# Stick-breaking scores copied to SBUF by ACT, sums in place, and a unit's turned weights asked for one unit later with a third buffer

## Chip, cores and metric

One Trainium2 chip, one core. The metric is the device time of one execution in microseconds (us), the median of three runs. Lower is better.

## What is computed

One layer of a hybrid decoder on 512 tokens of width 2048, in float32. A combined projection of the normalised input gives two groups of 16 heads of 64: group A is sliding-window attention, group B is stick-breaking attention. Both outputs are normalised, go through one output projection and are added to the input; an MLP with a squared ReLU (2048 to 8192 to 2048) follows. The change touches group B, which is this for each head:

```
z        = q . k / sqrt(64)                       # 512 x 512, strictly causal
log_beta = log_sigmoid(z)
log_1m   = where(causal, log_sigmoid(-z), 0)
later    = cumsum(log_1m, reversed) - log_1m      # along the keys
w        = where(causal, exp(log_beta + later), 0)
out      = w @ v
```

## The kernel before

Every large product is made of three TensorE products of float32r parts (`mm3`, lines 123 to 125): each operand is split by ACT (the high part, line 91) and DVE (the low part, line 92). The time has four stages: group A's and B's projections and attention, the output projection (`out_group`, tiles `ps_o`), the up products (`ps_u`) and the down products (`ps_d`).

The attention has no stage of its own. It is spread between the products of the projections. A group of products (`group_T`, `v_group`, `out_group`) calls `pump()` after every 12 of them; a call is a tick here. On odd ticks `pump` begins a unit if one is due, on even ticks it ends an earlier one. A unit of group B (`sb_pair`) is one block of 128 queries of a pair of heads (s = 0 and 1), so that a pair has four units, i = 0 to 3, with w = 128, 256, 384 and 512 keys.

- `begin(i)`: six products give the scores `z` (line 558) of both heads, in two PSUM banks. ACT makes Abs, Exp and Ln (lines 571 to 573), DVE max(z, 0) + Ln (line 574, reading `z`), POOL masks the diagonal block (line 575), DVE scans from the end (line 578) and subtracts the sum from the scores (line 580, reading `z` once more), POOL masks again (line 581), and ACT takes Exp (line 583). The result is tile `b`.
- `end(i)`: TensorE turns the weights by transposes (`wtr`, line 592), DVE copies them to SBUF (`wt`, line 593). After i = 3 the weights meet the values (`bv`, line 609), and `finish_o` takes the squares and stores the output.

`pa` has four PSUM banks. The scores, the turned weights, `bv` and the small products of other helpers take them in turn, so a unit's scores take the two banks of the unit before, and the turned weights the two between. A bank is given out again when its last reader is done: for the scores that is line 580. A unit is ended on the tick after the next one has begun, which is three ticks after its own beginning. Within a group of 16 ticks eight units run, that is two pairs; the units of one pair of pairs begin 11 ticks after its q and k are projected. In the tick where a group of projections ends, its q and k are also evacuated by DVE (line 328), split by ACT (line 323) and POOL (line 324).

The order of instructions on each engine is fixed before the run by a planner. It starts from the order of the program but may put later instructions first where it reckons that an earlier one has to wait.

Of the kernel before, what the change touches and what calls it, by code (L numbers as in the profile page):

```python
# [12 lines left out]
F32 = mybir.dt.float32  # L13
F32R = mybir.dt.float32r
AF = mybir.ActivationFunctionType
ALU = mybir.AluOpType
# [4 lines left out]
P = 128  # L21
T = 512
# [36 lines left out]
def hymba_layer(ctx: ExitStack, tc: tile.TileContext, x, norm_attn_g, w_in, q_norm_g, k_norm_g,  # L59
                sinks, rel_bias, swa_out_g, sb_out_g, w_out, norm_mlp_g, w_up, w_down, sel, eye, out):  # L60
    nc = tc.nc
    x, out = x[0], out[0]
# [21 lines left out]
    wk = attn.enter_context(tc.tile_pool(name="wk", bufs=2, side="right"))  # L84
# [44 lines left out]
    nc.scalar.dma_start(out=ident, in_=eye)  # L129
    NG = 50  # L130
    gT = const.tile([P, NG], F32, name="gT")
    gin = wk.tile([16, P], F32, tag="wb", name="gin")
    nc.scalar.dma_start(out=gin, in_=norm_attn_g.rearrange("o (k p) -> (o k) p", p=P))


# [26 lines left out]

    def xsquares(n, xb):
        for t in range(NT):
            junk = wk.tile([P, 512], F32, tag="wd", name=f"jx{n}_{t}")
            nc.scalar.activation(out=junk, in_=xb[:, t], func=AF.Square, accum_out=ss1[:, t, n:n + 1])

    kv_parts = []
# [45 lines left out]
    nc.vector.memset(c15, 1.5)  # L214
    ones2 = const.tile([P, 2], F32, name="ones2")
    nc.vector.memset(ones2, 1.0)
    bo32 = wk.tile([P, P], F32, tag="wb", name="bo32")
    nc.vector.memset(bo32, 0.0)
    for s in range(2):
        nc.vector.memset(bo32[s * DH:(s + 1) * DH, s * DH:(s + 1) * DH], 1.0 / DH)  # L220
# [56 lines left out]
    chains, units, flight, clock = [], deque(), deque(), [0]  # L277
# [5 lines left out]
    def pump():  # L283
        clock[0] += 1
        chains[:] = [g for g in chains if next(g, None) is not None]
        if clock[0] % 2:
            begun = bool(units) and units[0][0] <= clock[0]
            if begun:
                begin, end = units.popleft()[1]
                begin()  # L290
                flight.append(end)
            flight.append(None) if not begun and flight else None
        elif len(flight) > 1:
            end = flight.popleft()
            if flight[0] is None:
                flight.clear()
            end()

    def drain():
        while units or flight:  # L300
# [30 lines left out]
    def normed(ps, gcol, name):  # L331


        qf = evacuated(ps, 1.0, name)
        o = qkp.tile([P, 2, T], F32R, tag="qk", name=f"hl_{name}")

        def chain():
            sq = wk.tile([P, T], F32, tag="wb", name=f"sq_{name}")
            nc.scalar.square(out=sq, in_=qf)
            sh = wk.tile([P, T], F32R, tag="wc", name=f"sh_{name}")  # L340
            nc.scalar.copy(out=sh, in_=sq)
            sl = wk.tile([P, T], F32R, tag="wd", name=f"sl_{name}")
            nc.vector.tensor_tensor(out=sl, in0=sq, in1=sh.bitcast(F32), op=ALU.subtract)
            for _ in range(CHAIN):
                yield True
            mp = bank(f"mp_{name}")
            nc.tensor.matmul(mp, bo, sh, start=True, stop=False)
            nc.tensor.matmul(mp, bo, sl, start=False, stop=True)
            y = wk.tile([P, T], F32, tag="wc", name=f"y_{name}")
            t1 = wk.tile([P, T], F32, tag="wd", name=f"qt_{name}")  # L350
            nc.scalar.activation(out=y, in_=mp, func=AF.Ln, scale=LN_SCALE, bias=epsb)
            nc.scalar.activation(out=y, in_=y, func=AF.Exp, scale=-0.5, bias=lnb)
            nc.scalar.square(out=t1, in_=y)
            nc.vector.scalar_tensor_tensor(out=t1, in0=mp, scalar=EPS, in1=t1, op0=ALU.add, op1=ALU.mult)
            nc.scalar.activation(out=t1, in_=t1, func=AF.Identity, scale=-0.5, bias=c15)
            nc.vector.scalar_tensor_tensor(out=qf, in0=qf, scalar=gT[:, gcol:gcol + 1], in1=y,
                                           op0=ALU.mult, op1=ALU.mult)
            nc.vector.tensor_tensor(out=qf, in0=qf, in1=t1, op=ALU.mult)
            hilo(qf, o)

        g = chain()
        next(g)
        chains.append(g)
        return o
# [60 lines left out]
    def swa_pair(g, m, q, turned):  # L425
        c = 4 * g + m
# [26 lines left out]
        def softmax(hf, sc):  # L453
            prs = []
            bt = bias[0]
            for s in range(2):
                h = heads[s]
                pr = wk.tile([P, 2, 256], F32, tag=("wa", "wb")[s], name=f"pr{c}_{hf}{s}")
                scv = sc[s].rearrange("p (n k) -> p n k", n=2)
                if hf == 0:  # L460
                    nc.gpsimd.memset(pr[:, 0, 0:P], NEG)
                    nc.vector.tensor_tensor(out=pr[:, 0, P:], in0=scv[:, 0, P:], in1=bt[:, s, P:], op=ALU.add)
                    nc.vector.tensor_tensor(out=pr[:, 1], in0=scv[:, 1], in1=bt[:, s], op=ALU.add)
                else:
                    nc.vector.tensor_tensor(out=pr, in0=scv,
                                            in1=bt[:, s:s + 1].broadcast_to([P, 2, 256]), op=ALU.add)
                mx = sm.tile([P, 2], F32, tag="mx", name=f"mx{c}_{hf}{s}")
                nc.vector.tensor_reduce(out=mx, in_=pr, axis=AX.X, op=ALU.max)
                nm = sm.tile([P, 2], F32, tag="nm", name=f"nm{c}_{hf}{s}")
                nc.vector.tensor_scalar(out=nm, in0=mx, scalar1=sink[:, h:h + 1], scalar2=-1.0,  # L470
                                        op0=ALU.max, op1=ALU.mult)
                den = sm.tile([P, 2], F32, tag="den", name=f"den{c}_{hf}{s}")
                es = sm.tile([P, 2], F32, tag="es", name=f"es{c}_{hf}{s}")
                for nn in range(2):
                    nc.scalar.activation(out=pr[:, nn], in_=pr[:, nn], func=AF.Exp, bias=nm[:, nn:nn + 1],
                                         accum_out=den[:, nn:nn + 1])
                nc.scalar.activation(out=es, in_=nm, func=AF.Exp, bias=sink[:, h:h + 1])
                nc.vector.tensor_tensor(out=den, in0=den, in1=es, op=ALU.add)
                nc.vector.reciprocal(out=den, in_=den)
                for nn in range(2):  # L480
                    nc.gpsimd.tensor_scalar(out=pr[:, nn], in0=pr[:, nn], scalar1=den[:, nn:nn + 1],
                                            scalar2=1.0, op0=ALU.mult, op1=ALU.mult)
                prs.append(pr)
            return prs
# [31 lines left out]
                                         start=(j == 0), stop=(j == 3))  # L516
                finish_o(av, 0, 4 * g + 2 * s + m // 2)

        return [(partial(begin, hf), partial(end, hf)) for hf in range(2)]

    qperm = (lambda st: st.rearrange("p (s m d) -> p m s d", s=2, m=4, d=DH),
             lambda st: st.rearrange("p (m s d) -> p m s d", s=2, m=4, d=DH))
# [26 lines left out]
    def sb_pair(c, q, k, vs, keep):  # L549
# [12 lines left out]
        def weights(i, sc):  # L562
            w = (i + 1) * P
            dg = slice(i * P, (i + 1) * P)
            ws = []
            for s in range(2):
                z = sc[s][:, 0:w]
                a = wk.tile([P, 512], F32, tag=("wa", "wc")[s], name=f"a{c}_{i}{s}")[:, 0:w]
                b = wk.tile([P, 512], F32, tag=("wb", "wd")[s], name=f"b{c}_{i}{s}")[:, 0:w]

                nc.scalar.activation(out=a, in_=z, func=AF.Abs)
                nc.scalar.activation(out=a, in_=a, func=AF.Exp, scale=-1.0)
                nc.scalar.activation(out=a, in_=a, func=AF.Ln, bias=1.0)
                nc.vector.scalar_tensor_tensor(out=b, in0=z, scalar=0.0, in1=a, op0=ALU.max, op1=ALU.add)
                nc.gpsimd.affine_select(out=b[:, dg], in_=b[:, dg], pattern=[[-1, P]], compare_op=ALU.is_gt,
                                        fill=0.0, base=0, channel_multiplier=1)

                nc.vector.tensor_tensor_scan(out=a[:, ::-1], data0=ones2[:, 0:1].broadcast_to([P, w]),
                                             data1=b[:, ::-1], initial=0.0, op0=ALU.mult, op1=ALU.add)
                nc.vector.tensor_tensor(out=b, in0=z, in1=a, op=ALU.subtract)  # L580
                nc.gpsimd.affine_select(out=b[:, dg], in_=b[:, dg], pattern=[[-1, P]], compare_op=ALU.is_gt,
                                        fill=NEG, base=0, channel_multiplier=1)
                nc.scalar.activation(out=b, in_=b, func=AF.Exp)
                ws.append(b)
            return ws
# [27 lines left out]
            if o is not None:  # L613
                ohl[1, c] = o

        return [(partial(begin, i), partial(end, i)) for i in range(4)]

    ohl = {}

# [5 lines left out]
    for o in range(2):  # L625
        vs = v_group(o)
        for hq in range(2):
# [12 lines left out]
            for pr, (q, k) in enumerate(((q0, k0), (q1, k1))):  # L640
                c = 2 * qd + pr
# [284 lines left out]
    wd = w_down.rearrange("(g r p) n -> r p g n", r=2, p=P)  # L926
# [135 lines left out]
    for cj in range(2 * NC):  # L1062
        c, j = divmod(cj, 2)
# [7 lines left out]
        for s, (name, ai, _, b, more) in enumerate(d_products(cj)):  # L1071
# [33 lines left out]
            if not more:  # L1105
                pool, tag = ((pa, "pa"), (pp, "pp"))[b // 2]
                banks[b] = [pool.tile([P, 512], F32, tag=tag, name=f"ps_d{q}{tt}") for tt in range(2)]
            a = act[c, ai]

            at_end = q == 14 * NC - 1  # L1110
            for h, tt in sorted(((h, tt) for h in range(2) for tt in range(2)), key=lambda x: x[::-1] if at_end else x):
# [3 lines left out]
                for kk in range(2):  # L1115
                    al, ar = a[:, 0, 2 * h + kk, ts], a[:, 1, 2 * h + kk, ts]
                    first, end = h == 0 and kk == 0 and not more, h == 1 and kk == 1
# [36 lines left out]
```

## Time and profile before

| | |
|---|---|
| median of 3 runs | 1998.48 us (1997.99 to 2000.78) |
| the profiled execution's own time | 1998.97 us |
| its span, first to last instruction | 1997.2 us |
| TensorE busy | 1976.4 us, 99% |
| DVE, ACT, POOL busy | 1649.4, 1037.5, 1011.3 us |
| group B's units, first scores to last `bv` | about 320 to 629 us of the span |

A span is time on the core; the run's own time is 1.8 us longer. Products overlap each other by a part of their duration, so that two products of 0.39 us follow each other every 0.23 us. A gap is therefore best read from start to start.

### The profile page before, as it was taken

The page shows a single profiled execution, that of the slowest core. Times are in us where ns is not written, and L with a number is a line of the kernel's source. Part 1 is how long each engine was busy: PE and PEld are TensorE (multiplying, and loading weights), DVE is VectorE, ACT ScalarE, POOL GpSimd, SP SyncE. Part 2 cuts the span into 40 slices and gives each one's busy share as a digit, 9 for nine tenths or more (in the row PEclk, how much of TensorE's full clock was granted, in tenths as well). Part 3 has the DMA queues.
Part 4 walks back from the last instruction along what each step waited for, and adds up shares of the span by engine and source line. Part 5 has one row for each costly group of instructions (what it writes and reads, how often), then busy time and mean ns, then how long its engine had stood idle before and what let it go on. Part 6 is the DMA issues. An engine that isn't in the chain of part 4 may idle for free.

```text
span 1997.2 us, 31358 instructions
## 1 busy us (share of the span) xinstructions
PE 1976.4 (99%) x11652; PEld 1717.5 (86%) x11652; DVE 1649.4 (83%) x2142; ACT 1037.5 (52%) x1900; POOL 1011.3 (51%) x898
## 2 busy tenths in 40 slices
PE   8999999999999999999999999999999999999999
PEld 7887787778777889999999999998888888888887
DVE  4469654664776479999999999999999999999997
ACT  6357544453554575656565656565443333333444
POOL 0013431221321038777777777776866656656653
PEclk9999999999999999999999999999999999999999
DMA  6732332224245555665656565656766457456451
GB/s 224 146 119 80 100 98 83 75 69 137 93 140 172 192 169 180 217 201 189 208 181 215 180 216 181 212 176 245 290 250 250 158 221 291 161 221 261 143 204 67
DMA packets 213916, 350.31 MB, mean 175 GB/s; under 512 B 9779, under 2 KB 154372, under 8 KB 206596
## 3 DMA queue, kind: packets, MB, share of 16 engines
q1 hardware_dynamic: 211216, 345.02, 51.0%
q10 hardware_dynamic: 2548, 3.30, 1.3%
q8 instruction: 91, 1.49, 0.3%
q14 instruction: 61, 0.50, 0.1%
HBM read 270.16 MB, written 78.12 MB: 174 GB/s over the span
## 4 chain that ended last, share of the span: by engine, by line
PE 89%; DVE 5%; ACT 3%; POOL 1%; issue 1%; DMA 1%; POOLq 0%; SPq 0%; DVEq 0%; ACTq 0%
PE ps_u L831 11%; PE ps_u L830 11%; PE ps_u L832 11%; PE ps_d L1119 9%; PE ps_d L1120 9%; PE ps_d L1118 9%; PE ps_qk L123 3%; PE ps_qk L125 3%; PE ps_qk L124 3%; PE ps_o L125 2%; PE ps_o L123 2%; PE ps_o L124 2%; PE ps_qa L123 1%; PE ps_qa L124 1%; PE ps_qa L125 1%; DVE lo_d L92 1%
## 5 line engine op out<-in xcount | busy, mean ns | idle before, releaser
L832 PE MATMUL ps_u<-h2h,lo_u 128*128 128x256 f32 x1792 | 507.5, 283 | 0.1
L830 PE MATMUL ps_u<-h2h,hi_u 128*128 128x256 f32 x1792 | 507.6, 283 | 0.0
L831 PE MATMUL ps_u<-h2l,hi_u 128*128 128x256 f32 x1792 | 507.4, 283 | 0.0
L1118 PE MATMUL ps_d<-hi_d,ad 128*128 128x512 f32 x896 | 348.8, 389 | 2.7 <-ACT e L856 2.7
L1119 PE MATMUL ps_d<-lo_d,ad 128*128 128x512 f32 x896 | 349.0, 390 | 0.1
L1120 PE MATMUL ps_d<-hi_d,ad 128*128 128x512 f32 x896 | 348.7, 389 | 0.0
L832 PEld LDWEIGHTS ps_u<-h2h,lo_u 128*128 128x128 f32 x1792 | 344.1, 192 | 0.3 <-DVE lo_u L92 0.3
L831 PEld LDWEIGHTS ps_u<-h2l,hi_u 128*128 128x128 f32 x1792 | 344.2, 192 | 0.0
L830 PEld LDWEIGHTS ps_u<-h2h,hi_u 128*128 128x128 f32 x1792 | 344.1, 192 | 0.0
L806 POOL TENSOR_TENSOR s_u<-st_u 128x256 f32<-128x256 f32 x256 | 212.1, 849 | 245.1 <-DVE lo_u L92 176.3
L965 POOL TENSOR_TENSOR T<-st_d,T 128x1024 f32<-128x1024 f32 x64 | 174.2, 2724 | 188.3 <-DVE lo_d L92 185.8
L92 DVE TENSOR_TENSOR lo_d<-T,hi_d 128x1024 fp32r<-128x1024 f32 x128 | 250.5, 1971 | 19.5 <-ACT hi_d L91 18.9
L92 DVE TENSOR_TENSOR lo_u<-s_u,hi_u 128x512 fp32r<-128x512 f32 x256 | 261.8, 1023 | 0.3 <-ACT hi_u L91 0.3
L91 ACT CAST hi_u<-st_u 128x384 fp32r<-128x384 f32 x256 | 131.2, 513 | 229.4 <-PE ps_u L831 224.1
L91 ACT CAST hi_d<-T 128x1024 fp32r<-128x1024 f32 x128 | 134.9, 1055 | 188.5 <-PE ps_d L1120 175.6
L92 DVE TENSOR_TENSOR lo_u<-st_u,hi_u 128x384 fp32r<-128x384 f32 x256 | 196.1, 766 | 30.4 <-ACT hi_u L91 29.5
L1118 PEld LDWEIGHTS ps_d<-hi_d,ad 128*128 128x128 f32 x896 | 168.2, 188 | 38.0 <-ACT e L856 3.1
L1119 PEld LDWEIGHTS ps_d<-lo_d,ad 128*128 128x128 f32 x896 | 168.2, 188 | 36.1 <-DVE lo_d L92 1.3
L1120 PEld LDWEIGHTS ps_d<-hi_d,ad 128*128 128x128 f32 x896 | 168.2, 188 | 34.8
L92 DVE TENSOR_TENSOR lo_d<-st_d,hi_d 128x1024 fp32r<-128x1024 f32 x96 | 189.7, 1988 | 9.1 <-ACT hi_d L91 9.0
L91 ACT CAST hi_d<-st_d 128x1024 fp32r<-128x1024 f32 x96 | 101.3, 1056 | 154.3 <-PE ps_d L1120 135.4
L91 ACT CAST hi_u<-s_u 128x512 fp32r<-128x512 f32 x256 | 158.5, 619 | 18.0 <-POOL s_u L806 18.0
(242 smaller groups left out, 3818.9 us busy)
## 6 DMA issues: line engine op xcount, KB each, us to landing
st_u<-in_w_up SPq DMA_DIRECT2D x128, 512.0 KB, 3.7
st_d<-in_w_down SPq DMA_DIRECT2D x64, 1024.0 KB, 8.3
ad<-ac SPq DMA_DIRECT2D x56, 1024.0 KB, 6.3
ac<-ah SPq DMA_DIRECT2D x32, 896.0 KB, 4.0
ac<-al SPq DMA_DIRECT2D x32, 896.0 KB, 5.8
st_qk<-in_w_in SPq DMA_DIRECT2D x64, 256.0 KB, 3.0
st_o<-in_w_out SPq DMA_DIRECT2D x32, 512.0 KB, 4.2
st_qa<-in_w_in SPq DMA_DIRECT2D x16, 512.0 KB, 4.0
```

The lines of the kernel that those rows point to most:

```text
L91: cast = nc.scalar.copy(out=hi, in_=st)
L92: nc.vector.tensor_tensor(out=lo, in0=st, in1=hi.bitcast(F32), op=ALU.subtract)
L123: nc.tensor.matmul(ps, ah, bh, start=first, stop=False)
L124: nc.tensor.matmul(ps, ah, bl, start=False, stop=False)
L806: last_sum[0] = nc.gpsimd.tensor_tensor(out=o, in0=a, in1=b, op=op)
L830: nc.tensor.matmul(o, wh[:, a], hh[:, b], start=first, stop=False, skip_group_check=True)
L831: nc.tensor.matmul(o, wh[:, a], hl[:, b], start=False, stop=False, skip_group_check=True)
L832: nc.tensor.matmul(o, wl[:, a], hh[:, b], start=False, stop=(k == KP - 1), skip_group_check=True)
L965: nc.gpsimd.tensor_tensor(out=o, in0=raw[cj, a, h], in1=raw[cj, b, h], op=ALU.subtract)
L1118: nc.tensor.matmul(o, al, bh[:, kk], start=first, stop=False, skip_group_check=True)
L1119: nc.tensor.matmul(o, al, bl[:, kk], start=False, stop=False, skip_group_check=True)
L1120: nc.tensor.matmul(o, ar, bh[:, kk], start=False, stop=end, skip_group_check=True)
```

## The change

Each unit now begins with an ACT copy of both heads' scores from PSUM to tile `b` in SBUF. Line 574 still reads `z` in PSUM, but writes in place to `a`; the first mask and the scan work in `a` too; the subtraction takes its scores from `b` and no longer from PSUM. A unit carries a number (`ahead`): a group A unit is ended when more than one is in flight, as before, a group B unit when more than two are. So on the ticks at which one of group B ended unit u, it now ends the one before it. Tags `wb` and `wd`, in which `b` lies, have three buffers and not two; the other users of these tags are given the same number.

```
@@ pump
             if begun:
-                begin, end = units.popleft()[1]
+                begin, end, ahead = units.popleft()[1]
                 begin()
-                flight.append(end)
+                flight.append((ahead, end))
             flight.append(None) if not begun and flight else None
-        elif len(flight) > 1:
+        elif flight and len(flight) > (flight[0] or (0,))[0]:
             end = flight.popleft()
-            if flight[0] is None:
+            if flight and all(f is None for f in flight):
                 flight.clear()
-            end()
+            if end:
+                end[1]()
@@ softmax (group A; the same for gin, jx, bo32, sq, sl and qt: bufs=3)
-                pr = wk.tile([P, 2, 256], F32, tag=("wa", "wb")[s], name=f"pr{c}_{hf}{s}")
+                pr = wk.tile([P, 2, 256], F32, tag=("wa", "wb")[s], bufs=2 + s, name=f"pr{c}_{hf}{s}")
@@ swa_pair
-        return [(partial(begin, hf), partial(end, hf)) for hf in range(2)]
+        return [(partial(begin, hf), partial(end, hf), 1) for hf in range(2)]
@@ weights (group B)
-                b = wk.tile([P, 512], F32, tag=("wb", "wd")[s], name=f"b{c}_{i}{s}")[:, 0:w]
+                b = wk.tile([P, 512], F32, tag=("wb", "wd")[s], bufs=3, name=f"b{c}_{i}{s}")[:, 0:w]
+                nc.scalar.copy(out=b, in_=z)
...
-                nc.vector.scalar_tensor_tensor(out=b, in0=z, scalar=0.0, in1=a, op0=ALU.max, op1=ALU.add)
-                nc.gpsimd.affine_select(out=b[:, dg], in_=b[:, dg], pattern=[[-1, P]], compare_op=ALU.is_gt,
+                nc.vector.scalar_tensor_tensor(out=a, in0=z, scalar=0.0, in1=a, op0=ALU.max, op1=ALU.add)
+                nc.gpsimd.affine_select(out=a[:, dg], in_=a[:, dg], pattern=[[-1, P]], compare_op=ALU.is_gt,
                                         fill=0.0, base=0, channel_multiplier=1)
...
-                                             data1=b[:, ::-1], initial=0.0, op0=ALU.mult, op1=ALU.add)
-                nc.vector.tensor_tensor(out=b, in0=z, in1=a, op=ALU.subtract)
+                                             data1=a[:, ::-1], initial=0.0, op0=ALU.mult, op1=ALU.add)
+                nc.vector.tensor_tensor(out=b, in0=b, in1=a, op=ALU.subtract)
@@ sb_pair
-        return [(partial(begin, i), partial(end, i)) for i in range(4)]
+        return [(partial(begin, i), partial(end, i), 2) for i in range(4)]
```

## Rows read from the trace of the kernel before

**Rows 1.** By stretch: PE, PEld, DVE, ACT, POOL busy us, clock, DMA share, GB/s.
```profile
340.00:360.00 20.00, 17.67 (x82) 12.47 (x82) 14.82 (x25) 9.62 (x22) 5.98 (x12) 0.91 0.20 56
500.00:520.00 20.00, 18.68 (x90) 13.88 (x89) 15.47 (x24) 12.82 (x28) 8.71 (x12) 1.00 0.20 58
300.00:640.00 340.00, 333.27 (x1602) 254.43 (x1601) 217.29 (x350) 171.14 (x352) 78.24 (x147) 0.99 0.34 106
```

**Rows 2.** What TensorE waited for: us in total, times, longest.
```profile
PE z L558 <- DVE b L580: 3.6, 6, 0.7
...
PE z L558 <- DVE wt L593: 1.5, 2, 0.8
PE wtr L592 <- ACT b L583: 1.0, 2, 0.8
```

**Rows 3.** Timeline, a unit of 512 keys and the scores behind it: start, us, engine.
```profile
375.53 1.09 PE L558 MATMUL z<-hl_b,hl_b 64*128 64x512 f32 x6
375.60 0.99 ACT L583 ACTIVATE b<-b 128x384 f32<-128x384 f32 x2 [2.09 <-POOL b L581]
...
376.55 0.50 PE L123 MATMUL ps_v<-hi_v,hT 128*128 128x512 f32 x1
...
379.21 1.29 DVE L574 SCALAR_TENSOR_TENSOR b<-z,a 128x512 f32<-128x512 f32 x2 [1.80 <-ACT a L573]
...
379.59 1.05 ACT L91 CAST hi_qk<-st_qk 128x1024 fp32r<-128x1024 f32 x1
...
382.89 1.26 DVE L580 TENSOR_TENSOR b<-z,a 128x512 f32<-128x512 f32 x2
383.61 1.21 PE L558 MATMUL z<-hl_b,hl_b 64*128 64x256 f32 x6 [0.64 <-DVE b L580]
384.75 0.50 PE L123 MATMUL ps_v<-hi_v,hT 128*128 128x512 f32 x1
```

**Rows 4.** Timeline, a unit of 256 keys.
```profile
362.18 0.62 PE L558 MATMUL z<-hl_b,hl_b 64*128 64x256 f32 x6
362.73 0.51 PE L123 MATMUL ps_v<-hi_v,hT 128*128 128x512 f32 x1
...
366.73 0.73 DVE L580 TENSOR_TENSOR b<-z,a 128x256 f32<-128x256 f32 x2
367.38 0.48 DVE L593 COPY wt<-wtr 128x128 f32<-128x128 f32 x2
```

**Rows 5.** Timeline, the end of a pair's last unit.
```profile
387.61 1.04 PE L592 MATMUL wtr<-ident,b 128*128 128x128 f32 x8
...
388.25 1.29 DVE L593 COPY wt<-wtr 128x512 f32<-128x512 f32 x2
...
388.72 0.40 PE L124 MATMUL ps_v<-lo_v,hT 128*128 128x512 f32 x1
...
389.04 2.91 PE L609 MATMUL bv<-wt,v 128*64 128x512 f32 x16
```

**Rows 6.** Timeline, units that begin as a group's q and k are split.
```profile
337.59 1.30 POOL L324 TENSOR_TENSOR hl_b<-f_b,hl_b 128x512 fp32r<-128x512 f32 x1
337.69 2.02 DVE L578 TENSOR_TENSOR_SCAN a<-ones,b 128x384 f32<-128x384 f32 x1
...
339.63 0.53 DVE L574 SCALAR_TENSOR_TENSOR b<-z,a 128x384 f32<-128x384 f32 x1
...
340.62 0.96 DVE L578 TENSOR_TENSOR_SCAN a<-ones,b 128x384 f32<-128x384 f32 x1
340.68 0.50 PE L558 MATMUL z<-hl_b,hl_b 64*128 64x512 f32 x1 [0.66 <-DVE b L580]
...
343.27 0.79 PE L123 MATMUL ps_v<-hi_v,hT 128*128 128x512 f32 x1
...
345.57 0.45 PE L125 MATMUL ps_v<-hi_v,hT 128*128 128x512 f32 x1
```

**Rows 7.** A group of instructions: busy us, mean ns of one.
```profile
L388 ACT COPY o<-bv 128x512 f32<-128x512 f32 x6 | 3.5, 581 | 0.0
```

More of the change, by code (lines that the diff above doesn't have):

```diff
@@ L131, in hymba_layer @@
     gT = const.tile([P, NG], F32, name="gT")
-    gin = wk.tile([16, P], F32, tag="wb", name="gin")
+    gin = wk.tile([16, P], F32, tag="wb", bufs=3, name="gin")
     nc.scalar.dma_start(out=gin, in_=norm_attn_g.rearrange("o (k p) -> (o k) p", p=P))
@@ L164, in xsquares @@
         for t in range(NT):
-            junk = wk.tile([P, 512], F32, tag="wd", name=f"jx{n}_{t}")
+            junk = wk.tile([P, 512], F32, tag="wd", bufs=3, name=f"jx{n}_{t}")
             nc.scalar.activation(out=junk, in_=xb[:, t], func=AF.Square, accum_out=ss1[:, t, n:n + 1])
@@ L216, in hymba_layer @@
     nc.vector.memset(ones2, 1.0)
-    bo32 = wk.tile([P, P], F32, tag="wb", name="bo32")
+    bo32 = wk.tile([P, P], F32, tag="wb", bufs=3, name="bo32")
     nc.vector.memset(bo32, 0.0)
@@ L337, in chain @@
         def chain():
-            sq = wk.tile([P, T], F32, tag="wb", name=f"sq_{name}")
+            sq = wk.tile([P, T], F32, tag="wb", bufs=3, name=f"sq_{name}")
             nc.scalar.square(out=sq, in_=qf)
@@ L341, in chain @@
             nc.scalar.copy(out=sh, in_=sq)
-            sl = wk.tile([P, T], F32R, tag="wd", name=f"sl_{name}")
+            sl = wk.tile([P, T], F32R, tag="wd", bufs=3, name=f"sl_{name}")
             nc.vector.tensor_tensor(out=sl, in0=sq, in1=sh.bitcast(F32), op=ALU.subtract)
@@ L349, in chain @@
             y = wk.tile([P, T], F32, tag="wc", name=f"y_{name}")
-            t1 = wk.tile([P, T], F32, tag="wd", name=f"qt_{name}")
+            t1 = wk.tile([P, T], F32, tag="wd", bufs=3, name=f"qt_{name}")
             nc.scalar.activation(out=y, in_=mp, func=AF.Ln, scale=LN_SCALE, bias=epsb)
```

## The prediction

> **What bounds the kernel now.** I read the busy table first: TensorE is busy 99% of the span, so a change can only win what TensorE loses. The table by stretch shows where. In the 340 us in which group B's units run between the projections, TensorE is busy 333.27 us, so 6.7 us are open idling, and none of the other engines is near full: DVE 217, ACT 171, POOL 78 [rows 1]. In one stretch the granted clock is 0.91 as well [rows 1]. Open idling understates a loss, since two products overlap; so I then read the table of waits for who is late, and the timeline for how much from start to start.
>
> The waits name three releasers within the units: the subtraction of line 580 (6 times), the copies of the turned weights (twice), the last Exp (twice) [rows 2]. The subtraction is the last reader of a score bank, so the scores of the next unit wait for a chain of DVE work. The reader is to see this in [rows 3]: a unit of 512 keys starts at 375.53; the subtractions of its two heads start at 382.89 and take 1.26; the next scores start at 383.61 after 0.64 us of idling, and then take 1.14 until the next product, where the same six took 0.55 when nothing held them [rows 4]: the second head waits for the second subtraction.
>
> **What the change removes.** First, the hold of the bank by line 580. Its last reader is now line 574. That line isn't early by itself: it comes after Abs, Exp and Ln, and the copies stand ahead of these. With T the start of a unit of 512 keys, the pair of line 574 ends at 379.21 + 1.29 = 380.50, T + 4.97 [rows 3]. A copy from PSUM to SBUF by ACT of 512 columns took 0.58 [rows 7]; two back to back, about 0.1 of overlap, add 1.06: T + 6.03. Without the wait the next scores would come at 383.61 - 0.64 = 382.97, T + 7.44. So there is 1.4 us to spare, and the wait goes: 0.64 + (1.14 - 0.55) = 1.23 us a place. I count the places from the order of ticks and the timeline: behind the last unit of the second and third pair of each run of four pairs, that is four (383.61 is the first) of the six waits in the table; the other two are at edges [rows 2, 3]. 4 x 1.23 = 4.9 us.
>
> The two edges are where units begin while a group's q and k are split. At the first the scores of 512 keys idle 0.66 before 340.68 and then take 343.27 - 340.68 = 2.59, where they took 376.55 - 375.53 = 1.02 elsewhere [rows 3, 6]; and five products from 343.27 to 345.57 take 2.30, where an undisturbed twelve took 387.61 - 384.75 = 2.86, so five 1.19: half the clock, 1.2 of 2.4 GHz, after TensorE had waited [rows 3, 5, 6]. Loss 0.66 + 1.57 + 1.11 = 3.3. After the change the second head's line 574 ends at 339.63 + 0.53 = 340.16, plus two copies of 384 columns; two ACT instructions of that width took 0.99 [rows 3, 6], so 341.1. The second head wants its bank 0.1 after 340.0, so 1.0 stays, and I take the clock to hold: 2.3 saved. The second edge idles 1.32 in its stretch at full clock [rows 1]; for the hidden part of such a wait I add 0.4, and with 1.0 staying 0.7 is saved. Edges: 3.0 us.
>
> Third, the last units at the edges: the transposes wait 1.0 us for the last Exp [rows 2]. They are asked for two ticks, some 6 us, later: 1.0 us.
>
> Removed: 4.9 + 3.0 + 1.0 = 8.9 us.
>
> **What it adds.** 64 copies on ACT, of 128 to 512 columns, at most 64 x 0.58 = 37 us of an engine that is idle 169 of these 340 us [rows 1, 7]. Behind them in ACT's order stand the unit's own Abs and the casts of the weights' chunks. A cast waits for products four chunks back and is wanted some three chunks later, so a delay of 1 us reaches nobody. Without that cover each cast would hold the products. The subtraction, the mask and the scan keep their number, width and engine. The third buffer of `b` is given back by the transposes one tick before the next copy into it; group A's tiles under these tags only gain one. The last pair ends two ticks later, at tick 158 of 160 and one tick before the fetch that looks for its result, so nothing is left for the drain.
>
> The moved step is `end`. It issues transposes, two DVE copies and, once a pair, `bv`, which can't start before the copies. DVE takes these copies behind the subtractions of the unit begun on the tick before: the copies at 367.38 start as the subtractions that began at 366.73 end [rows 4]. Before, the pair's last `end` met a next unit of 128 keys. Now it meets one of 256 keys. There the second subtraction ended at 367.46, T + 5.28 with T = 362.18 [rows 4]; two ACT copies of 256 columns add about 0.6: T + 5.9. One copy of 512 columns takes 1.29 / 2 = 0.65 [rows 5], so `bv` can start at T + 6.5. The transposes start 0.55 + 2.86 after T, and `bv` comes 389.04 - 387.61 = 1.43 behind their start with two products in between [rows 3 to 5]: T + 4.85. That gap is 1.6 us if the planner still puts two products there. The two products in [rows 5] are its doing, though: it filled the wait for the copies there to within the normal step (0.32 from 388.72 to 389.04), and up to ten products are left to fill with. It was wrong by 1.2 us at the scores behind 512 keys and right at 128, so at 256 I take 0.3, for the bounds 0 and 1.6. It concerns six of eight pairs, as the last pair before each lead-out meets no unit: 6 x 0.3 = 1.8 us.
>
> DVE's two masks and scans show one more thing. The scan of 384 columns at 337.69 took 2.02 beside a POOL subtraction of 1.30, and 0.96 at 340.62 [rows 6]. The Trainium skill, "SBUF — State Buffer", section "Who interferes with whom", states that a DVE instruction with two SBUF inputs contends with a GpSimd instruction that reads SBUF, and that the second to issue fully blocks. By that rule, with which the row agrees, the change puts line 580 among those that block, since it had one input in PSUM; by that rule alone the sum would be that of the ports rival below.
>
> **Sum.** 8.9 - 1.8 = 7.1 us. The profiled execution took 1998.97; less 7.1 is 1991.9. The median shown is 0.5 below the profiled run, so I predict 1991.4 us.
>
> **Rivals.**
>
> *ACT's order eats the earlier bank.* Line 574 still reads `z` in PSUM, so the copy by itself frees nothing. If the planner puts the earlier unit's two Exps (0.99) and a cast (1.05) ahead of the copies [rows 3], the second head's line 574 ends at T + 6.03 + 2.04 = T + 8.07, and 0.6 stays at each of four places; at the edges another 1.0 each. 8.9 - 2.4 - 2.0 - 1.8 = 2.7 us: 1995.8. For it: ACT did take those Exps as the 512 unit began. Against: the cast then stood behind Ln.
>
> *`bv` waits, at full clock.* All of the 1.6 in six pairs, 9.6 us: 8.9 - 9.6 = -0.7, 1999.2. For it: the planner's error at the scores. Against: the filling in [rows 5].
>
> *`bv` waits and the clock falls.* As above, and after each such wait the clock halves as it did after 340.68, at 1.1 us [rows 6]: 6 x 2.7 = 16.2, so 7.3 slower, 2005.8. From 8.9 / 6 = 1.5 us of loss a pair the change is slower than before, from 2.15 measurably so. For it: one wait in two pieces of about a microsecond brought the clock down. Against: the 0.64 us waits, four of them, did not.
>
> *Ports.* Line 580 now stands behind POOL's subtractions at the edges as the scan did, 2.02 - 0.96 = 1.06 for each head at two edges [rows 6], 4.2 us at most, and what stands behind it comes late by as much: 8.9 - 1.8 - 4.2 = 2.9, 1995.6. Against: nothing of the scores waits for line 580 any more, and the turned weights have two ticks more.
>
> **How the numbers follow.** A difference of 0.2%, 4 us, is about what a measurement of this kernel can tell from none. Chances: forecast 0.60 (its own range, with `bv` from 0 to 0.6 a pair, 1989 to 1995); ACT's order 0.12, `bv` at full clock 0.08, ports 0.08, all three within 4 us of 1998.48; `bv` with the clock 0.12. So faster 0.60, same 0.28, slower 0.12. Low end: no cost at `bv` and both edges clean (2.0 more), 8.9 + 2.0 = 10.9, 1987.6, rounded out to 1986.5 for the hidden parts of short waits. High end: 2000, which takes in the three middle cases and leaves out the slow one.
>
> **What would show it.** Right: no wait of `z` for line 580; scores behind 512 keys at the normal step from the product before, and 0.55 long; transposes without a wait for Exp; more than two products between the transposes of i = 3 and `bv`; TensorE busy at least 337 of the 340 us; clock 1.00 throughout. Wrong: `z` waiting for line 574, long starts of `bv` behind the copies, or a stretch with a lower clock. Time won in group B but lost later would be wrong in another way: the stages behind are as full as before, so I take them to move up unchanged.

## The result, and the profile after

The changed kernel is slower: 2015.83 us, median of six runs (2011.80 to 2019.79), against 1999.14 for the kernel before (six runs, 1997.87 to 2000.86); ratio 1.008, interval [1.007, 1.009]. The forecast was 1991.4 us in a range from 1986.5 to 2000.

The profiled execution of the changed kernel took 2013.05 us, its span is 2011.3. The loss lies where the gain was expected: from the first scores of group B to the last small product of the second branch's scale (`rs`) it is 321.16 to 658.9, 337.7 us, where the kernel before needed 320.29 to 645.3, 325.0 us. That is 12.7 of the 14.1 us by which the spans differ.

The lines are numbered anew: scores `z` L559, the copy L571, Abs, Exp, Ln L573 to L575, max L576, first mask L577, scan L580, subtraction L582, second mask L583, last Exp L585, transposes L594, copies of the turned weights L595, values `bv` L611. First, as in [rows 2], what TensorE waited for between 300 and 680 us:

```profile
PE bv L611 <- DVE wt L595: 12.7, 7, 2.9
PE wtr L594 <- DVE a L576: 3.9, 2, 2.5
PE rs L650 <- DVE a L576: 1.6, 1, 1.6
PE z L559 <- DVE wt L595: 0.3, 1, 0.3
PE z L559 <- DVE a L576: 0.2, 1, 0.2
```

All three releasers of [rows 2] are nearly gone: no scores wait for the subtraction, no transposes for the last Exp. In their place the values wait for the copies of the turned weights, before seven of the eight `bv`. Behind the two edges (the transposes at 353.80, `rs` at 529.65) and once between pairs (555.02) TensorE waits for the max, which still reads `z`. Summed, 18.7 us are waited here, where the same view of the kernel before has 6.4.

By stretch, as in [rows 1] (PE, PEld, DVE, ACT, POOL busy us, clock, DMA share, GB/s; the clock is the mean granted in the stretch, and 0.91 means that a part of the 20 us ran at 1.2 GHz and the rest at 2.4):

```profile
340.00:360.00 20.00, 17.50 (x88) 13.14 (x87) 14.94 (x24) 11.72 (x28) 7.29 (x14) 1.00 0.18 54
360.00:380.00 20.00, 17.14 (x78) 11.27 (x77) 9.21 (x17) 10.12 (x23) 2.28 (x7) 0.91 0.20 66
...
520.00:540.00 20.00, 18.44 (x91) 14.07 (x90) 15.13 (x29) 12.09 (x30) 7.52 (x14) 0.91 0.18 53
540.00:560.00 20.00, 16.91 (x83) 11.39 (x82) 12.68 (x23) 14.42 (x32) 4.27 (x9) 1.00 0.29 99
```

No other engine is near full, ACT neither. So it looks like lateness, not load. One pair's end shows it (timeline: start, us, engine, line; in brackets the idle time before it and what ended it). It answers to [rows 4, 5]:

```profile
393.28 0.76 PE L559 MATMUL z<-hl_b,hl_b 64*128 64x256 f32 x6
393.48 1.03 ACT L91 CAST hi_qk<-st_qk 128x1024 fp32r<-128x1024 f32 x1
394.42 0.31 ACT L585 ACTIVATE b<-b 128x128 f32<-128x128 f32 x1
394.68 0.28 DVE L582 TENSOR_TENSOR b<-b,a 128x128 f32<-128x128 f32 x1
395.12 0.29 POOL L583 TENSOR_SCALAR_AFFINE_SELECT b<-b 128x128 f32<-128x128 f32 x1 [1.08 <-DVE b L582]
395.44 0.31 ACT L585 ACTIVATE b<-b 128x128 f32<-128x128 f32 x1 [0.72 <-POOL b L583]
395.66 0.36 ACT L571 COPY b<-z 128x256 f32<-128x256 f32 x1
396.87 1.03 PE L594 MATMUL wtr<-ident,b 128*128 128x128 f32 x8
397.49 0.42 DVE L576 SCALAR_TENSOR_TENSOR a<-z,a 128x256 f32<-128x256 f32 x1 [0.93 <-ACT a L575]
398.98 0.40 DVE L576 SCALAR_TENSOR_TENSOR a<-z,a 128x256 f32<-128x256 f32 x1
400.62 0.66 DVE L595 COPY wt<-wtr 128x512 f32<-128x512 f32 x1
401.33 3.30 PE L611 MATMUL bv<-wt,v 128*64 128x512 f32 x16 [2.29 <-DVE wt L595]
401.54 0.68 DVE L595 COPY wt<-wtr 128x512 f32<-128x512 f32 x1
```

The scores of a 256-key unit start at T = 393.28, but ACT first reads them at 395.66, T + 2.38. In ACT's order a cast (393.48) and the 128-key unit's last Exps stand ahead of the copy, and before the second head's Exp it sits idle for POOL's mask until 395.44. The max follows at T + 4.21, the copy of the turned weights, which DVE takes behind this unit's max and scan, at T + 7.34, and `bv` at T + 8.05. TensorE was done with the transposes and the five products that stand between them and `bv` some 2.3 us earlier.

### The profile page after: what moved, and what is told of

The parts are those of the page before. It is cut to its first block, busy times and chain, and to the rows that moved or that the text cites. A ratio compares the mean times of both kernels' runs of the same rounds, so it can differ in the third digit from the quotient of the medians.

```text
span 2011.3 us, 31417 instructions
## 1 busy us (share of the span) xinstructions
PE 1978.0 (98%) x11652; PEld 1716.1 (85%) x11652; DVE 1649.8 (82%) x2142; ACT 1059.6 (53%) x1964; POOL 1012.4 (50%) x898
## 4 chain that ended last, share of the span: by engine, by line
PE 87%; DVE 5%; ACT 3%; POOL 2%; issue 2%; DMA 1%; POOLq 0%; DVEq 0%; SPq 0%; ACTq 0%
PE ps_u L834 10%; PE ps_u L833 10%; PE ps_u L832 10%; PE ps_d L1121 10%; PE ps_d L1120 10%; PE ps_d L1122 10%; PE ps_qk L123 2%; PE ps_qk L125 2%; PE ps_qk L124 2%; PE ps_o L125 2%; PE ps_o L123 2%; PE ps_o L124 2%; PE ps_qa L123 1%; PE ps_qa L124 1%; PE ps_qa L125 1%
## 5 line engine op out<-in xcount | busy, mean ns | idle before, releaser
L92 DVE TENSOR_TENSOR lo_d<-T,hi_d 128x1024 fp32r<-128x1024 f32 x128 | 250.8, 1973 | 19.3 <-ACT hi_d L91 18.7
```

The source lines that it names most:

```text
L92: nc.vector.tensor_tensor(out=lo, in0=st, in1=hi.bitcast(F32), op=ALU.subtract)
```

## The experiments

Twelve kernels ran in three groups, each beside the kernel before, whose medians were 1999.67, 1999.37 and 1999.54 us. Theory E: the later end brings a pair's `bv` behind the DVE work of a 256-key unit. Theory A: the copies on ACT make a unit's chain late, since they stand behind the earlier unit's last Exp. "Lag" below is the time from a unit's first score product to ACT's first read of these scores, read off the timeline for all 32 units. In the kernel before its mean is 0.96 us, in the changed one 1.93 (0.65 to 5.62).

**The parts of the change, one by one.** a1 has the copies without the late end:

```
-        return [(partial(begin, i), partial(end, i), 2) for i in range(4)]
+        return [(partial(begin, i), partial(end, i), 1) for i in range(4)]
```

> The changed kernel with the end of a unit where it was before (ahead 1): copies, sums in place and third buffers alone. Theory E (the later end brings the values' product bv behind the DVE work of a unit of 256 keys, where the planner puts only five products between): the 12.7 us of waits of bv for the turned weights' copies go, 1990 to 2001 us. Theory A (the ACT copies make each unit's chain late, since ACT takes them in order behind the earlier unit's last Exp): the time stays at 2006 us or more, and transposes wait for Exp.

2024.01 us, ratio 1.0118 [1.0101, 1.0135]: the slowest of all. Its waits (us, times, longest):

```profile
PE wtr L594 <- ACT b L585: 19.4, 12, 3.3
...
PE bv L611 <- DVE wt L595: 0.5, 2, 0.3
```

This is theory A's case. The copies make the chain late by themselves (the lag is 1.81 us in the mean); with the end on the next tick the transposes pay, not `bv`. a2 has the late end and the third buffers without copies (sums and subtraction as in the kernel before):

```
-                nc.scalar.copy(out=b, in_=z)
-                nc.vector.tensor_tensor(out=b, in0=b, in1=a, op=ALU.subtract)
+                nc.vector.tensor_tensor(out=b, in0=z, in1=a, op=ALU.subtract)
```

> The kernel before with the end of a unit one unit later and the third buffers, no copies, scores read from PSUM as before. Theory E: bv waits as in the changed kernel, in its order four products stand between transposes and bv, six waits of 1.5 to 2.5 us, 2006 to 2018 us. Theory A: without the copies the chain is early enough, bv waits under 0.5 us each, 1993 to 2002 us.

2010.27 us, 1.0051 [1.0036, 1.0066]. Its waits:

```profile
PE z L559 <- DVE b L581: 7.8, 7, 1.5
PE bv L610 <- DVE wt L594: 3.2, 6, 0.5
...
```

The late end costs as well, by both places: `bv` waits 0.5 us a pair, and the scores wait longer for the subtraction than before. The time lies in theory E's range, but each wait of `bv` is far below the 1.5 to 2.5 us that E named: without the copies the chain is early (lag 1.09 us). b2 has only the sums in place and the third buffers, with the end as before:

> The kernel before with nothing but the sums in place: the difference still reads the scores in their bank, writes the buffer that the last Exp then rewrites; no copies, the end one unit later as before (not two), though with three buffers. Both theories: nothing that PE waits for is changed, so 1997 to 2001 us, ratio 0.999 to 1.001. A time above 2003 us would say that the third buffers or the reuse cost something by themselves, and that both theories put the loss in the wrong place.

2000.45 us, 1.0007 [0.9997, 1.0016]: nothing, with the waits of the kernel before (3.8 us of the scores for the subtraction). The third buffers and the sums in place are free.

**Two repairs.** a3 is the changed kernel with the values two ticks later, behind the scores of the unit after (`pump` takes them from `later`):

```
+            if c % 4 == 3:
+                values()
+            else:
+                later.append(values)
```

> The changed kernel with bv asked for two ticks after its transposes (24 products and the next scores between) in the six pairs that have a unit behind them. Theory E: no wait of bv for copies is left in these, 12 us and the lost clock come back, 1990 to 2002 us; what is left are the waits at the two edges, about 4 us of transposes and 1.6 us of rs for line 576. Theory A: DVE's lateness only moves, scores or transposes wait for copies instead, 2006 us or more.

1996.28 us, 0.9984 [0.9974, 0.9993]. What is left of the waits:

```profile
PE bv L621 <- DVE wt L599: 3.4, 1, 3.4
PE wtr L598 <- DVE a L580: 2.5, 1, 2.5
PE rs L660 <- DVE a L580: 1.6, 1, 1.6
```

The first is a pair whose values aren't moved, the others stand behind the edges. The lag is no better, 2.22 us in the mean. So the chain stays late, but nothing of TensorE's stands close behind it any more. This came out as theory E had it; A had looked for 2006 us or more. a4 keeps `bv` where it is and puts a unit's last Exps on ACT behind the next unit's Ln (`release` issues the Exps of the unit before):

```
-                nc.scalar.activation(out=b, in_=b, func=AF.Exp)
...
+            release(ln)
+            held.append(ws)
```

> The changed kernel with a unit's last Exp held back on ACT until the next unit's Ln is issued, so that the copies never stand behind it; bv as in the changed kernel, five products behind its transposes. Theory A: the chain starts some 2 us sooner, bv no longer waits, 1990 to 2001 us. Theory E: a wait of about 0.5 to 1.5 us stays at each of six bv, and the time falls by less than half of what was lost, 2004 to 2013 us.

1995.34 us, 0.998 [0.997, 0.9989]. The same place as above, in this kernel:

```profile
385.91 0.62 PE L567 MATMUL z<-hl_b,hl_b 64*128 64x256 f32 x6
386.56 0.37 ACT L579 COPY b<-z 128x256 f32<-128x256 f32 x1 [1.26 <-PE z L567]
389.05 0.49 ACT L556 ACTIVATE b<-b 128x128 f32<-128x128 f32 x2
391.55 0.66 DVE L604 COPY wt<-wtr 128x512 f32<-128x512 f32 x1
392.27 3.30 PE L622 MATMUL bv<-wt,v 128*64 128x512 f32 x16 [0.72 <-DVE wt L604]
```

The copy starts at T + 0.65 and not T + 2.38, the turned weights are copied at T + 5.64 and not T + 7.34, `bv` starts at T + 6.36 and not T + 8.05. All three are earlier by 1.7 us: whatever stood ahead of the copies is the lateness of `bv`, and the rest of the chain is as long as it was. The lag's mean falls to 0.89 us, the waits of `bv` from 12.7 to 4.7 us:

```profile
PE bv L622 <- DVE wt L604: 4.7, 7, 0.9
```

So neither theory holds alone. The chain is late by ACT's order (A: a1 and a4), and the lateness costs what it does because the later end has put `bv` close behind that chain (E: a3). With the copies on time, E's own share is the 0.7 us a pair. The cast that stood among the Exps runs at 384.27 here, before the scores, so a4 doesn't tell its share from theirs.

**Other accounts of the late chain.** In the changed kernel the two heads are out of step (copy, Abs, copy, Exp, Abs, ...), so DVE takes one head's chain ahead of the other's max. d1 writes every operation over both heads:

```
             for s in range(2):
...
-                nc.scalar.copy(out=b, in_=z)
...
-                nc.scalar.activation(out=a, in_=z, func=AF.Abs)
...
+                nc.scalar.copy(out=ws[s], in_=zs[s])
+            for s in range(2):
+                nc.scalar.activation(out=av[s], in_=zs[s], func=AF.Abs)
...
```

> The changed kernel, with the unit's operations written operation by operation over its two heads (copy, copy, Abs, Abs, Exp, Exp, Ln, Ln; max, max; scan, scan; difference, difference; last Exps), where the changed kernel writes head by head. Earlier units' last Exps still stand where the planner puts them, ahead of the copies; six products instead of five stand between the last turned scores and the values. If what costs the time is that the two heads fall out of step (VectorE takes one head's whole chain before the other's max), the waits of the values for the last copy of turned weights should go from 12.7 us (7 waits) to under 4 us, and the time to 1995 to 2000 us. If the cost is that the copies stand behind the earlier unit's last Exp, whatever the order of the heads, the values' waits stay at 8 to 13 us and the time is 2006 to 2018 us. The extra product alone is worth at most 6 x 0.2 us.

2011.13 us, 1.0063 [1.0046, 1.0079]. The heads are in step and the wait of the same pair's `bv` is the same to a hundredth (the view ends at 402 us and shows 12 of its 16 products):

```profile
391.76 0.62 PE L559 MATMUL z<-hl_b,hl_b 64*128 64x256 f32 x6
393.61 0.56 ACT L590 ACTIVATE b<-b 128x128 f32<-128x128 f32 x2 [1.57 <-POOL b L587]
394.07 0.63 ACT L571 COPY b<-z 128x256 f32<-128x256 f32 x2
399.90 2.37 PE L615 MATMUL bv<-wt,v 128*64 128x512 f32 x12 [2.29 <-DVE wt L599]
```

Over all pairs:

```profile
PE bv L615 <- DVE wt L599: 12.6, 6, 3.9
```

The copies start at T + 2.31, again behind the earlier unit's Exps, and the waits of `bv` are as long as in the changed kernel, so that account of them falls. (Of the 4.7 us by which d1 is faster than the changed kernel a part lies inside `bv`: its 16 products took 2.89 us to the next instruction here, 3.23 there.) b1 moves the copies behind Ln:

```
-                nc.scalar.copy(out=b, in_=z)
                 nc.scalar.activation(out=a, in_=z, func=AF.Abs)
...
                 nc.scalar.activation(out=a, in_=a, func=AF.Ln, bias=1.0)
+                nc.scalar.copy(out=b, in_=z)
```

> The changed kernel with each copy of the scores moved from ahead of Abs to behind Ln: the in-place difference and the later end stay, ScalarE does the same work, but the chain Abs, Exp, Ln no longer waits for the copy. If the copies' 0.58 us at the head of each chain is what makes it late, the values' waits shrink from 12.7 us to about 5 us and the time is 1997 to 2004 us. If it is the earlier unit's last Exp in front of whatever comes first (copy or Abs), the waits stay near 12 us and the time is 2008 to 2018 us; the bank of the scores is given back some 2 us later then, and waits of the scores for the copy may be added.

2018.56 us, 1.0098 [1.0083, 1.0113], a little above the range named; `bv` waits 12.1 us in 7. The 0.58 us of a copy ahead of Abs aren't it either: ACT's first read, now Abs, comes 2.07 us behind the scores in the mean. Whatever read the scores first was late. a5 lets the max read the copy, so that Abs is the bank's last reader:

```
-                nc.vector.scalar_tensor_tensor(out=a, in0=z, scalar=0.0, in1=a, ...)
+                nc.vector.scalar_tensor_tensor(out=a, in0=b, scalar=0.0, in1=a, ...)
```

> The changed kernel with VectorE's max and sum reading the copy instead of the bank of the scores, so that the bank is given back by ScalarE's Abs. What waits for the max in the changed kernel (wtr 3.9 us in 2, rs 1.6 us in 1, z 0.2) should go: 5.7 us and the lower clock behind the two waits at the edges. If the edges' banks are a part of the loss by themselves, the time is 2006 to 2011 us, with the values' waits still near 12 us. If they are only where a chain that is late anyway shows, the waits go over to the turned scores or the values and the time is 2012 to 2018 us.

2017.74 us, 1.0091 [1.0076, 1.0106]. The waits for the max are gone, and those of `bv` grow to 17.4 us. The banks that the max held are only where a late chain shows first.

**Both repairs.** c1 is a3 and a4 together.

> The changed kernel with both repairs that each gave back the loss alone: a unit's last Exps stand on ScalarE behind the next unit's Ln, and the values of a pair with a unit behind it are asked for two steps later, behind that unit's scores. If each repair removes its own part (the late chain; the short distance of the values from the last copy), the two add: the values' waits go to 0.9 us or less at the last pair alone, and the time is 1991 to 1994 us. If they are two ways to the same 17 to 20 us (the values' waits and the clock that falls behind them), there is nothing left to add and the time is 1994.5 to 1997 us, as with either alone.

1985.37 us, 0.9933 [0.9918, 0.9948]: 14 us faster than the kernel before, 10 us faster than either repair alone, and more than expected. So they aren't two ways to the same gain. A part that had not been counted lies inside `bv`: in a4 its 16 products take 3.23 us from their start to TensorE's next instruction, with the second head's copy ending during them. In c1 they take 2.31, which makes 5.5 us in six pairs. The waits between 300 and 680 us fall from 6.0 us in a4 to 2.1. c1's one wait between 300 and 660 us, and its stretches beside [rows 1]:

```profile
PE bv L632 <- DVE wt L608: 2.1, 1, 2.1
```

```profile
340.00:360.00 20.00, 20.00 (x102) 15.85 (x102) 18.05 (x31) 14.57 (x35) 7.05 (x16) 1.00 0.27 80
...
500.00:520.00 20.00, 20.00 (x106) 15.56 (x105) 17.51 (x35) 16.65 (x40) 9.75 (x16) 1.00 0.26 79
...
600.00:620.00 20.00, 17.84 (x83) 13.00 (x81) 14.40 (x20) 10.99 (x18) 1.87 (x4) 0.92 0.50 154
```

TensorE doesn't idle from 300 to 600 us. c4 is c1 without the copies:

> c1 without the copies: last Exps behind the next unit's Ln, values two steps later, end two units later, sums in place, but the difference reads the scores in their bank again (as in the kernel before and in a2, where the scores waited 7.8 us in 7 waits for the difference). If the copies are what frees the banks and c1's gain over the kernel before is that, the scores' waits for the difference come back at 4 to 8 us and the time is 1993 to 2000 us. If the copies are worth nothing once the other two are in (the late end alone takes the waits away), the time is 1984 to 1987 us, as c1.

2002.69 us, 1.0015 [1.0005, 1.0024]:

```profile
PE z L571 <- DVE b L592: 7.8, 6, 2.0
PE wtr L605 <- DVE b L592: 1.3, 4, 0.4
...
```

Without the copies the scores wait for the subtraction again, and all of c1's gain is lost (17.3 us between the two), a little more than expected. e1 is the kernel before, its sums in place as in b2, with the values two ticks later:

> The kernel before (no copies, end one unit later; sums in place as in b2) with only the values of a pair asked for two steps later. The kernel before shows no wait of the values at all, and b2 two of 0.2 us. If c1's gain belongs to the change once its losses are repaired, this is 1997 to 2001 us, with the scores' waits for the difference still at 3.5 us. If the repair is worth something without the change (the last copies of turned weights then hold nothing up), the time is 1990 to 1996 us, and the gain isn't the change's.

1998.86 us, 0.9995 [0.9986, 1.0005]: by the medians this repair is worth nothing by itself. Its trace, of the fastest of its ten executions (1997.26 us), has the stretch from the first scores to the last `rs` at 320.92 to 642.2, 321.3 us, 3.8 less than before. c2 is c1 with the edit of a5:

> c1 with the max reading the copy, as a5: the banks of the scores come back without VectorE. In c1 PE waits no more for the max (one wait is left between 300 and 660 us, 2.1 us of the last pair's values). So if waits tell it all, 1984 to 1987 us, as c1. If the max runs faster from SBUF than from PSUM, VectorE gains some 0.1 us each and nothing changes; if two SBUF inputs hold POOL's masks up (1.13 us instead of 0.29 beside such an instruction in the changed kernel), the chain is slower and the time is 1986 to 1990 us.

1985.17 us, 0.993 [0.9916, 0.9945], the same as c1.

## Why the prediction was wrong

**The removals were right, and worth at least what was forecast.** The waits of [rows 2] went. With the new losses repaired (c1) the stretch from the first scores to the last `rs` takes 319.86 to 631.4, 311.5 us, 13.5 less than before. By the traces 3.8 of these come with the values' move alone (e1), which leaves 9.7 for the copies, the later end and the order of Exp together, against 8.9 us forecast; by the medians of c1 and e1 it is 13.5. From one pair's `bv` to the next (before [rows 5] and this line; then c1, whose view ends at 426 us):

```profile
421.28 2.92 PE L609 MATMUL bv<-wt,v 128*64 128x512 f32 x16
394.08 2.37 PE L632 MATMUL bv<-wt,v 128*64 128x512 f32 x16
424.34 1.94 PE L632 MATMUL bv<-wt,v 128*64 128x512 f32 x10
```

The kernel before needs 32.24 us (389.04 to 421.28), e1 31.66 (393.46 to 425.12), c1 30.26. Most of e1's 0.58 lies in `bv` itself: from the start of its 16 products to TensorE's next instruction it took 2.84 before, where the second head's copy came during them, and 2.31 in e1 and c1. The other 1.40 the forecast had as 1.23. At the edges the scores wait no more in c1, as forecast.

**The step that failed is the cover of the copies on ACT.** It was worked out as if ACT began a unit's copies when it had begun Abs in the kernel before, T + 1.0 in the unit of [rows 3] and T + 0.65 in that of [rows 4]; the spare 1.4 us and "T + 5.9" both start from that, and the 169 us of idle ACT time were taken as cover. The two rows of the kernel before:

```profile
362.83 0.66 ACT L571 ACTIVATE a<-z 128x256 f32<-128x256 f32 x2 [1.97 <-PE z L558]
376.54 1.09 ACT L571 ACTIVATE a<-z 128x512 f32<-128x512 f32 x2
```

An idle engine is no cover when its idling is a wait at the head of its queue. ACT idled for POOL's mask with the earlier unit's last Exp in front, and the ready copies stood behind it. The sign was there: in [rows 3] the same Exps, at 375.60, come behind 2.09 us of such idling, with Abs behind them. The lag went from 0.96 to 1.93 us in the mean, with up to 5.62.

That case was in the text as the rival *ACT's order eats the earlier bank*, with 0.12, and its mechanism is the one that came. Its price was looked for mostly at the wrong place: at the scores (0.2 us waited for the max) and the edges (2.5 and 1.6 us waited behind them), and not at `bv`. There the chain on DVE stands ahead of the turned weights' copies, so that the delay of 1.7 us at ACT reached TensorE in full in the pair shown.

**The term that was mis-sized is the wait of `bv`,** 6 x 0.3 = 1.8 us within bounds 0 and 1.6 each. Measured: 12.7 us in 7, from 0.7 to 2.9; 1.2 of it at the last pair, which the forecast had left out. It has two parts. Undelayed, `bv` could start at T + 6.36 (a4), where T + 6.5 was forecast; the planner puts five products ahead of it, and 0.7 us stay a pair (4.7 us in 7 in a4): the forecast should have taken this, since a planner that misjudged the scores by 1.2 us was trusted here. The second part is the copies' lateness, 1.7 us in the pair shown, and this neither bound held, as both were worked out with copies on time. Beside the waits, `bv`'s own products took 3.23 us where they had taken 2.84, which no term of the sum had.

**The rival that came nearest** is *`bv` waits and the clock falls*, 2005.8 us with 0.12; the measured time is 10 us beyond it. In the profiled execution the clock fell twice: behind the first pair's waits (0.91 from 360 to 380 us; `bv` took 4.92 us to the next product where the next pair's took 3.23) and behind the 1.6 us before `rs` (0.91 from 520 to 540 us); behind 401.33 it stayed at 1.00. So here the larger size of each wait counts for more than the clock. But this is the second fastest of the six executions. Their granted clock over the whole span was 0.998 (this one) and 0.997 in the fastest, 0.995 in the two slowest, 0.9963 in the mean; in the kernel before, beside a1 to a4, it was 0.998 to 1.0, 0.9990 in the mean. If all lost clock is lost time, 0.0027 of 2015 us is some 5 us of the 16.7, an estimate from these means.

**Ports** show no price. The 128 masks on POOL had 52.8 us (33.1 and 19.7) between 318 and 640 us before and 51.7 (25.5 and 26.2) after: the first ones became faster, the second ones slower. The subtractions of 384 and 512 columns took 545 and 680 ns in the mean where they had taken 539 and 674, so the hold of 1.06 us that this rival reckoned with isn't seen. In c2, which gives the max a second SBUF input too, the masks take 58.5 us, in c1 53.1, and the time is the same. Single masks were held up, 1.15 us at 389.30, beside a subtraction of two SBUF inputs that DVE had begun at 389.08, against 0.29 for others. With that the rule cited ahead of the experiments (the Trainium skill, "SBUF — State Buffer", section "Who interferes with whom") agrees; its price is not in the time.

**What stays open.** Why lateness lasts from unit to unit is argued, not shown: before, the scores' wait for the bank held TensorE back until the chain had caught up; with the bank free, TensorE runs on, and one unit's late Exp makes the next unit's copies late. The share of the clock in the 16.7 us wasn't measured by itself. Not tried were the two ticks at the last pair, whose `bv` still waits 2.1 us in c1, and c1 with the end on the next tick, so that the later end's own share in the gain is not known.

## What to carry to other kernels

A copy that is to free a PSUM bank early does so only if its engine reaches it early: look at what stands ahead of it in that engine's order and what that instruction waits for, not at the engine's share of busy time. When a wait that throttled the leading engine goes, follow the same chain to its next consumer, and size the wait there in the new order with late links included. A change that loses may still be right in its aim: here the copies, the later end, the order of Exp and the later values gave 14 us together, while the copies alone cost 24, the values' move alone changed nothing that the medians tell, and all but the copies lost 3.

## What was not expected of the hardware

`bv`'s 16 products with 64 columns of weights took 2.31, 2.84 or 3.23 us from their start to TensorE's next instruction, at the full clock: 2.31 in c1 and e1, with both copies done; 2.84 before, with the second copy ending during them; 3.23 in the changed kernel, with a second stop for that copy inside the group, which the waits of TensorE's products don't list and its weight loads show:

```profile
402.27 0.20 PEld L611 LDWEIGHTS bv<-wt,v 128*64 128x64 f32 x4 [0.74 <-DVE wt L595]
```

The size of a wait didn't tell whether the granted clock fell. In the changed kernel it fell (0.91 in a stretch of 20 us, part of it at 1.2 and not 2.4 GHz) behind 2.50 us at the transposes of 353.80 and 2.86 us before `bv` at 365.55, and again behind 1.56 us at 529.65; it stayed at 1.00 in the stretch of 400 to 420 us with its 2.29 us. In the kernel before it fell behind the 0.66 us and the slow scores of [rows 6]. In c1 it fell behind one wait of 2.1 us at the last pair (0.92 from 600 to 620 us).
